# Layer 1's scale and shift by halves behind the last expert, and full fp32 products in gather and combine

## The chip, the cores and the metric

One core of a Trainium2 chip runs the kernel. The metric is the device time of one execution in microseconds (us). A run of the kernel before took 723.83 us in the median of three (722.95 to 725.26). TensorE, VectorE, ScalarE, GpSimd and SyncE are called PE, DVE, ACT, POOL and SP, as the profile calls them. SP issues the weight transfers.

## What is computed

Two layers, 256 tokens of width 1024, all in fp32. Both sub-layers of a layer normalise, scale and shift by vectors made from a conditioning row, and end in a gated residual with another normalisation:

```
for l in range(DEPTH):
    mod = cond @ w_mod[l] + b_mod[l]
    sh1, sc1, g1, sh2, sc2, g2 = split(mod, 6)
    h = layer_norm_plain(x) * (1 + sc1) + sh1
    y = concat(attention(q, k, v), pool(p)) @ w_out[l]      # q, k, v, p = split(h @ w_in[l])
    x = layer_norm_affine(ALPHA * x + g1 * y)
    h = layer_norm_plain(x) * (1 + sc2) + sh2
    y = grouped_moe(h)                                      # 16 experts, top 2 inside one group
    x = layer_norm_affine(ALPHA * x + g2 * y)
```

An expert is silu(h @ w_gate) * (h @ w_up) @ w_down with 512 inner columns. The weights of the 16 experts of one layer are 96 MB, so nearly all that is read from HBM is expert weights.

## The kernel before

**Weights.** `Stream` (line 35) holds a list of transfers in the order of use, mostly 1 MB each. It issues the next one on SP's queue whenever fewer than `limit` tiles are alive in a ring of 21 slots; `free` gives a tile back, `allow` moves the limit. A transfer into a slot waits for the last instruction that read it. The list stands in lines 114 to 169: for layer 0 the mixer's weights, `w_mod` in pieces v = 2, 4, 3, 5 (gate, scale, shift, gate), layer 1's scale piece (v = 1), eight pairs of experts (`add_pair`), and layer 1's shift piece (v = 0).

**Scale and shift.** `mod_mm` (line 290) multiplies the conditioning with one piece of `w_mod` on PE; `mod_fin` (line 327) copies the result, turns it by four PE transposes and reduces it on DVE. For layer 1, `mod_mm(l + 1, 1)` runs on PE in layer 0's mixer, between the two halves of the router's logits (line 719); its `mod_fin` runs in the second expert pair (line 1095). `mod_mm(1, 0)` runs behind the last expert of layer 0 (line 1145). Vectors v = 2, 4 and 3 are made on DVE instead, by `mod_dve` (line 353), eight operations each.

**Entry of layer 1.** `ready(t)` (line 1149) normalises 128 tokens on DVE, `enter` turns all eight 128-column pieces on PE and applies scale and shift on ACT or DVE; then `qk_mm` makes q and k in 16 products of 128x512 for that half of the tokens.

**Experts.** A pair i of experts passes through `gate_up` (line 907), `silu`, `act_t`, `down` (line 951) and `combine` (line 987); `combine(i - 1)` stands in pair i. Products of an expert use 64 columns of PE, so that the two experts of a pair lie side by side. Two calls per layer, `gather(0)` and `gather(4)` (line 868), collect the tokens of eight experts with a one-hot matrix. The normalised tokens are kept as a sum of two parts in float32r, `xh` and `xl`, made in `mixer` (lines 679 and 725 to 727), and each 128x512 product of the gather is made twice, once for each part:

```
for t in range(2):
    for xs in (xh, xl):
        T.matmul(b, xs[:, t, k * 128:(k + 1) * 128], SX[i][t], start=(n == 0), stop=(n == 3))
```

Likewise `down` splits an expert's output into `oh` and `ol` (lines 973 and 974: a cast on ACT and a subtraction on DVE), and `combine_mm` (line 982) multiplies both with the scatter matrix. `past` (line 1053) holds the case of more than 64 tokens on an expert, which this input does not take.

**Names.** In the profile `ps` is a PSUM bank, `wr` a ring slot, `s` a 128x512 work tile, `xn` and `hT` two large tiles that are reused (in the experts they hold `xh` and `xl`), `sT` the scatter matrix. L984 is `combine_mm`, L876 `gather`, L918 `gate_up`, L960 `down`, L455 `qk_mm`, L622 the output projection, L361 `mod_dve`, L297 `mod_mm`.

Of the kernel before, what the change touches and what calls it, by code (L numbers as in the profile page):

```python
# [8 lines left out]
F = mybir.dt.float32  # L9
BF = mybir.dt.bfloat16  # L10
FR = mybir.dt.float32r
# [5 lines left out]
D = 1024  # L17
# [56 lines left out]
def tile_trunk(ctx, tc, x, c, w_mod, b_mod, w_in, w_pool, pool_scale, w_out, ln1_g, ln1_b,  # L74
# [35 lines left out]

    def add_qk(l, q):
        st.add(("in", l, "qk", q), w_in[l].rearrange("(k p) n -> p k n", p=128)[:, 2 * q:2 * q + 2, 0:D])

    def add_in(l):
        w = w_in[l].rearrange("(k p) n -> p k n", p=128)
        if l:
            for q in range(4):
                add_qk(l, q)
# [38 lines left out]
    for l in range(DEPTH):  # L157
# [90 lines left out]
    def bias_cols():  # L248
# [6 lines left out]
        V.tensor_scalar(bcol[:, 0, :, 1], bcol[:, 0, :, 1], 1.0, None, op0=OP.add)  # L255
# [46 lines left out]
    col01 = const.tile([128, 2, 8], F, name="col01")  # L302
    colt[0, 0], colt[0, 1] = col01[:, 0], col01[:, 1]
# [15 lines left out]
    def mod01_fin(h, part):  # L319
# [3 lines left out]
        o = col01[:, :, 2 * h:2 * h + 2]  # L323
        V.reduce_sum(o, b[:, 0:256].rearrange("p (k v o r) -> p v k o r", k=2, v=2, o=2)[:, :, :, :, 0], axis=AX.X)
        V.tensor_add(o, o, bcol[:, 0, 2 * h:2 * h + 2, 0:2].rearrange("p k v -> p v k"))

# [104 lines left out]
    def enter(l, t, hT, xn):  # L431

        for h in range(2):
            b = ps()
            for k in range(4):
                kk = 4 * h + k
                T.transpose(b[:, k * 128:(k + 1) * 128], xn[:, t, kk * 128:(kk + 1) * 128], ident)
            for k in range(4):
# [4 lines left out]
                else:  # L443
                    A.activation(o, i, AF.Identity, scale=colt[l, 1][:, kk:kk + 1], bias=colt[l, 0][:, kk:kk + 1])

    def mixer(l, hT, xn, ready):
        pq = [[ps(), ps()] for _ in range(2)]

        def qk_mm(t, qs=range(4), kks=range(2)):
            for q in qs:  # L450
# [9 lines left out]
        if l:  # L460
            ready(0)
            qk_mm(0)
            ready(1)
        else:
# [11 lines left out]
        for t in range(2):  # L476
            if t:
                qk_mm(1, range(4) if l else (3,))
# [44 lines left out]
        for t in range(2):  # L523
            for n, dst in ((0, qT), (1, kT)):
# [3 lines left out]
                (A.copy if n else V.tensor_copy)(dst[:, :, t * 128:(t + 1) * 128], b.rearrange("p (c s) -> p c s", c=4))  # L528
# [76 lines left out]
        w = slot()  # L605
        xn2 = [w[:, t * D:(t + 1) * D] for t in range(2)]
        xnT = slot().rearrange("p (k s) -> p k s", k=8)
        st.allow(NS - 6)
# [24 lines left out]
        def norms_of(t):  # L633
            z = xn2[t]
# [14 lines left out]
        def turn(t):  # L649
            for h in range(2):  # L650
                b = ps()
                for k in range(4):
                    T.transpose(b[:, k * 128:(k + 1) * 128], xn2[t][:, (4 * h + k) * 128:(4 * h + k + 1) * 128], ident)
# [4 lines left out]
        xh = big.tile([128, 2, D], FR, name="xn")  # L658
# [20 lines left out]
        A.copy(xh[:, 0], xn2[0])  # L679
        mod_dve_fin(l, 3, acc[3])  # L680
        st.allow(NS - 3)
# [531 lines left out]
```

## Time and profile before

| what | value |
|---|---|
| median of 3 runs | 723.83 us |
| the profiled execution's own time | 724.93 us |
| its span, first to last instruction | 723.1 us |
| PE busy | 678.9 us (94%) |
| DVE busy | 326.8 us (45%) |
| ACT busy | 124.8 us (17%) |
| read from HBM | 278.59 MB, 387 GB/s over the span |
| mean granted PE clock | 0.986 |

The profiled execution is 1.1 us above the median. Times in rows count from the start of the span. A matmul's duration in a row is its latency; products that follow each other overlap, so the pace is read from the start of one to the start of the next. In a timeline row the first number is the start, the second the length; "x32" joins 32 records, and the bracket at the end tells how long the engine was idle before it and who released it.

### The profile page before, as it was taken

The page shows a single profiled execution, that of the slowest core. Times are in us where ns is not written, and L with a number is a line of the kernel's source. Part 1 is how long each engine was busy: PE and PEld are TensorE (multiplying, and loading weights), DVE is VectorE, ACT ScalarE, POOL GpSimd, SP SyncE. Part 2 cuts the span into 40 slices and gives each one's busy share as a digit, 9 for nine tenths or more (in the row PEclk, how much of TensorE's full clock was granted, in tenths as well). Part 3 has the DMA queues.
Part 4 walks back from the last instruction along what each step waited for, and adds up shares of the span by engine and source line. Part 5 has one row for each costly group of instructions (what it writes and reads, how often), then busy time and mean ns, then how long its engine had stood idle before and what let it go on. Part 6 is the DMA issues. An engine that isn't in the chain of part 4 may idle for free. (4 is left out here: it accounts for less than half of the span.)

```text
span 723.1 us, 8334 instructions
## 1 busy us (share of the span) xinstructions
PE 678.9 (94%) x3213; PEld 316.8 (44%) x3218; DVE 326.8 (45%) x582; ACT 124.8 (17%) x268; POOL 49.7 (7%) x76
## 2 busy tenths in 40 slices
PE   5999899999999999989979999998999999998994
PEld 2447555553333533423324575555333344342331
DVE  4008897662332532413153966666323243241305
ACT  1011432130110210121002035213210011012100
POOL 5001501100000000000010051010000000000002
PEclk9999999999999999999989999999999999999998
DMA  9999999999999999999999999767699999999992
GB/s 307 366 384 409 408 409 420 373 421 392 424 420 420 422 421 421 420 416 418 395 406 392 409 410 406 310 272 301 282 420 422 421 424 419 420 422 418 418 395 77
DMA packets 61729, 280.37 MB, mean 388 GB/s; under 512 B 5008, under 2 KB 14264, under 8 KB 38632
## 3 DMA queue, kind: packets, MB, share of 16 engines
q1 hardware_dynamic: 61040, 279.20, 96.1%
q8 instruction: 30, 0.49, 0.3%
q10 hardware_dynamic: 312, 0.32, 0.1%
q0 software_dynamic: 320, 0.14, 0.1%
q14 instruction: 27, 0.22, 0.1%
HBM read 278.59 MB, written 1.05 MB: 387 GB/s over the span
## 5 line engine op out<-in xcount | busy, mean ns | idle before, releaser
L918 PE MATMUL ps<-wr 128*64 128x512 f32 x1024 | 226.1, 596 | 0.0
L918 PEld LDWEIGHTS ps<-wr 128*64 128x64 f32 x1024 | 73.5, 138 | 147.2 <-issue 142.3
L960 PE MATMUL ps<-wr,s 128*64 128x512 f32 x512 | 113.8, 595 | 3.7 <-DVE s L945 2.9
L960 PEld LDWEIGHTS ps<-wr,s 128*64 128x64 f32 x512 | 35.5, 137 | 72.0 <-issue 63.8
L970 DVE SCALAR_TENSOR_TENSOR s<-ps,gc,gb 128x512 f32<-128x512 f32 x32 | 24.0, 748 | 84.0 <-PE ps L960 84.0
L455 PE MATMUL ps<-wr,hT 128*128 128x512 f32 x128 | 57.0, 597 | 0.4 <-ACT hT L429 0.2
L361 DVE SCALAR_TENSOR_TENSOR wr<-wr,condT 128x1024 f32<-128x1024 f32 x42 | 55.8, 1329 | 2.3 <-DMA wr<-in_w_mod_dram 0.9
L622 PE MATMUL ps<-wr,hT 128*128 128x512 f32 (+1 forms) x160 | 55.7, 507 | 0.1
L389 POOL TENSOR_TENSOR rs<-rs,mhalf 128x1 f32<-128x1 f32 x16 | 13.2, 823 | 554.1 <-DVE rs L388 554.1
L935 DVE TENSOR_TENSOR s<-s,ps 128x512 f32<-128x512 f32 x16 | 11.0, 687 | 86.5 <-PE ps L918 86.5
L973 ACT CAST wr<-s 128x512 fp32r<-128x512 f32 x30 | 18.5, 618 | 164.7 <-PE ps L918 107.7
L974 DVE TENSOR_TENSOR wr<-s,wr 128x512 fp32r<-128x512 f32 x30 | 20.8, 692 | 55.6 <-ACT wr L973 55.6
L622 PEld LDWEIGHTS ps<-wr,hT 128*128 128x128 f32 x160 | 30.2, 190 | 23.8 <-issue 21.5
L455 PEld LDWEIGHTS ps<-wr,hT 128*128 128x128 f32 x128 | 23.6, 190 | 28.9 <-issue 27.1
L984 PE MATMUL ps<-wr,sT 128*128 128x512 f32 x120 | 33.6, 413 | 0.0
L578 PE MATMUL ps<-wr,hT 128*128 128x512 f32 x64 | 28.3, 595 | 0.0
L504 PE MATMUL ps<-hT,wr 128*128 128x256 f32 x128 | 28.1, 380 | 0.0
L984 PEld LDWEIGHTS ps<-wr,sT 128*128 128x128 f32 x120 | 20.9, 189 | 16.3 <-issue 13.0
L933 DVE SCALAR_TENSOR_TENSOR s<-s,ps 128x512 f32<-128x512 f32 x16 | 11.0, 685 | 36.7 <-ACT s L932 36.7
L504 PEld LDWEIGHTS ps<-hT,wr 128*128 128x128 f32 x128 | 24.2, 190 | 4.5 <-issue 1.3
L876 PE MATMUL ps<-s,xn 128*128 128x512 f32 x64 | 25.4, 398 | 0.3 <-DVE s L854 0.3
L996 DVE TENSOR_TENSOR xt<-xt,ps 128x512 f32<-128x512 f32 x40 | 25.2, 683 | 0.5
(240 smaller groups left out, 611.5 us busy)
## 6 DMA issues: line engine op xcount, KB each, us to landing
wr<-in_w_gate_dram SPq DMA_DIRECT2D x64, 1024.0 KB, 19.3
wr<-in_w_up_dram SPq DMA_DIRECT2D x60, 1024.0 KB, 19.3
wr<-in_w_down_dram SPq DMA_DIRECT2D x56, 1024.0 KB, 19.5
wr<-in_w_mod_dram SPq DMA_DIRECT2D x48, 1024.0 KB, 15.1
wr<-in_w_in_dram SPq DMA_DIRECT2D x16, 1024.0 KB, 15.1
wr<-in_w_out_dram SPq DMA_DIRECT2D x8, 1024.0 KB, 18.7
wr<-in_w_down_dram SPq DMA_DIRECT2D x12, 512.0 KB, 11.1
wr<-in_w_up_dram SPq DMA_DIRECT2D x8, 512.0 KB, 17.4
```

What stands on the lines that cost most here:

```text
L361: V.scalar_tensor_tensor(acc, w[:, kk], condT[:, k, 0:1], acc, op0=OP.mult, op1=OP.add)
L455: T.matmul(pq[t][n], hT[:, k, t * 128:(t + 1) * 128], w[:, kk, n * 512:(n + 1) * 512], start=(k == 0), stop=(k == 7))
L504: T.matmul(pp[g // 2][:, (g % 2) * 256:(g % 2) * 256 + 256], w[:, kk, g * 128:(g + 1) * 128], hT[:, k, :], start=(k == 0 and g % 2 == 0), ...
L578: T.matmul(pv[t], hT[:, k, t * 128:(t + 1) * 128], w[:, kk, :], start=(k == 0), stop=(k == 7))
L622: T.matmul(py[t][-1][:, 0:c1 - c0], catT[:, k, t * 128:(t + 1) * 128], w[:, kk, n * 512 + c0:n * 512 + c1], start=(q == 2 and kk == 0), st ...
L876: T.matmul(b, xs[:, t, k * 128:(k + 1) * 128], SX[i][t], start=(n == 0), stop=(n == 3))
L918: T.matmul(bs[nm][64 * j:64 * j + 64, :], XE[i][k // 4][:, k % 4, c0:c0 + 64], st.get((nm, l, 2 * i + j, q))[:, k - k0, :], start=(k == 0) ...
L960: T.matmul(bo[n][64 * j:64 * j + 64, :], AT[i][:, k, 64 * j:64 * j + 64], st.get(("d", l, 2 * i + j, q))[:, k - k0, (n - n0) * 512:(n - n0 ...
L970: V.scalar_tensor_tensor(o, bo[n], GC[i], g2[:, c0], op0=OP.mult, op1=OP.mult)
L974: V.tensor_sub(ol[:, c0], o, oh[:, c0].bitcast(F))
L984: T.matmul(b, STt[i][:, t * 128:(t + 1) * 128], o[:, n * 512:(n + 1) * 512], start=(start and j == 0), stop=(stop and j == 1), skip_group_ ...
L996: V.tensor_add(b if i == NPAIR - 3 else xt[:, t, c0], xt[:, t, c0], b)
```

## The change

1. Gather and combine (also in `past`) lose the split into two parts: tokens and expert outputs stay fp32 and one fp32 product takes the place of two float32r ones. The two calls that split the tokens on ACT and DVE, and the cast and subtraction behind each expert, go; `down` writes its result straight into a tile `ob`.
2. Layer 1's scale and shift come by halves of 512 columns (both vectors together in `mod1`), all four transfers of a half side by side, both halves behind the last expert pair in the list, with layer 1's q and k weights between. `mod_mm(l + 1, 1)` in layer 0 goes, and PE gets seven `warm` products in that place, as layer 1 has now. `enter` turns and scales one half of the columns at a time, and the q and k products of layer 1 go by quarters.
3. In layer 0, the two copies of turned q behind the PE transposes move from DVE to ACT (`A.copy if n or not l`).
4. The ring's limits go up by one in two places, since the normalised tokens no longer take a slot.

```diff
+    def add_mod1(h):
+        w = w_mod[1].rearrange("(p k) n -> p k n", k=8)
+        for v in (1, 0):
+            for q in range(2):
+                st.add(("m1", h, v, q), w[:, 4 * q:4 * q + 4, v * D + h * 512:v * D + (h + 1) * 512])
...
         add_mod(l, 5)
-        if l + 1 < DEPTH:
-            add_mod(l + 1, 1)
         for i in range(NPAIR):
             add_pair(l, i)
         if l + 1 < DEPTH:
-            add_mod(l + 1, 0)
+            for q in range(4):
+                if q % 2 == 0:
+                    add_mod1(q // 2)
+                add_qk(l + 1, q)
...
+    def mod1(h):
+        acc = ps()
+        for k in range(8):
+            for v in range(2):
+                j = 2 * v + k % 2
+                T.matmul(acc[32 * j:32 * j + 32, :], condT[:, k, :], st.get(("m1", h, v, k // 4))[:, k % 4, :],
+                         start=(k < 2), stop=(k > 5))
+            if k % 4 == 3:
+                for v in range(2):
+                    st.free(("m1", h, v, k // 4))
+        part = s2()
+        A.copy(part, acc)
+        return part
...
         if l:
             ready(0)
-            qk_mm(0)
+            enter(l, 0, 0, hT, xn)()
+            qk_mm(0, (0, 1))
+            part = mod1(1)
             ready(1)
+            enter(l, 1, 0, hT, xn)()
+            mod1_fin(1, part)
+            fins = [enter(l, 0, 1, hT, xn)]
+            qk_mm(1, (0, 1))
+            fins.append(enter(l, 1, 1, hT, xn))
+            for fin in fins:
+                fin()
+            qk_mm(0, (2, 3))
...
-                (A.copy if n else V.tensor_copy)(dst[:, :, t * 128:(t + 1) * 128], b.rearrange("p (c s) -> p c s", c=4))
+                (A.copy if n or not l else V.tensor_copy)(dst[:, :, t * 128:(t + 1) * 128], b.rearrange("p (c s) -> p c s", c=4))
...
-        if l + 1 < DEPTH:
-            mod_mm(l + 1, 1)
         norms_of(1)
         exps(0)
-        if l + 1 == DEPTH:
-            warm(7)
-
-        V.tensor_sub(xl[:, 0], xn2[0], xh[:, 0].bitcast(F))
-        V.tensor_copy(xh[:, 1], xn2[1])
-        V.tensor_sub(xl[:, 1], xn2[1], xh[:, 1].bitcast(F))
+        warm(7)
...
                 for t in range(2):
-                    for xs in (xh, xl):
-                        T.matmul(b, xs[:, t, k * 128:(k + 1) * 128], SX[i][t], start=(n == 0), stop=(n == 3))
-                        n += 1
+                    T.matmul(b, X[:, t, k * 128:(k + 1) * 128], SX[i][t], start=(t == 0), stop=(t == 1))
...
-                    V.scalar_tensor_tensor(o, bo[n], GC[i], g2[:, c0], op0=OP.mult, op1=OP.mult)
-                    if last and n:
-                        break
-                    A.copy(oh[:, c0], o)
-                    V.tensor_sub(ol[:, c0], o, oh[:, c0].bitcast(F))
+                    V.scalar_tensor_tensor(O[i][:, c0], bo[n], GC[i], g2[:, c0], op0=OP.mult, op1=OP.mult)
...
         def combine_mm(i, t, n, b, start=True, stop=True):
-            for j, o in enumerate(O[i]):
-                T.matmul(b, STt[i][:, t * 128:(t + 1) * 128], o[:, n * 512:(n + 1) * 512],
-                         start=(start and j == 0), stop=(stop and j == 1), skip_group_check=not start)
+            T.matmul(b, STt[i][:, t * 128:(t + 1) * 128], O[i][:, n * 512:(n + 1) * 512],
+                     start=start, stop=stop, skip_group_check=not start)
...
-            if i == 1 and l + 1 < DEPTH:
-                mod_fin(l + 1, 1)
```

How the instructions stand now, at three places. First PE in layer 0's second expert pair (`L918`, now `L948`, is gate and up; `L984`, now `L1007`, the combine of the first pair; `L941`/`L971` and `L894`/`L924` transposes; `L335` the transposes of `mod_fin`). Before:

```order
L918 MATMUL ps<-wr 64x512 x32
L984 MATMUL ps<-wr,sT 128x512 x8
L941 MATMUL ps<-ident,s_1356 128x128 x4
L335 MATMUL ps<-ident,s_1381 128x128 x4
L894 MATMUL ps<-ident,s_1299 128x128 x4
L960 MATMUL ps<-wr,s_1379 64x512 x16
```

Now:

```order
L948 MATMUL ps<-wr 64x512 x32
L1007 MATMUL ps<-hT,sT 128x512 x4
L971 MATMUL ps<-ident,s_1311 128x128 x4
L924 MATMUL ps<-ident,s_1254 128x128 x4
L989 MATMUL ps<-wr,s_1330 64x512 x16
```

Eight combine products become four, of fp32, and the four transposes of `mod_fin` are gone. Second, PE where layer 1 makes q and k (`L437`, now `L465`, is `enter`; `L455`, now `L488`, the products; `L339` is `mod1`, `L351` `mod1_fin`). Before:

```order
L437 MATMUL ps<-ident,xn 128x128 x8
L455 MATMUL ps<-wr,hT 128x512 x16
L437 MATMUL ps<-ident,xn 128x128 x8
L455 MATMUL ps<-wr,hT 128x512 x16
L504 MATMUL ps<-hT,wr 128x256 x32
```

Now:

```order
L465 MATMUL ps<-ident,xn 128x128 x4
L488 MATMUL ps<-wr,hT 128x512 x8
L339 MATMUL ps<-wr,condT 32x512 x16
L465 MATMUL ps<-ident,xn 128x128 x4
L351 MATMUL ps<-ident,s_5180 128x128 x4
L465 MATMUL ps<-ident,xn 128x128 x4
L488 MATMUL ps<-wr,hT 128x512 x8
L465 MATMUL ps<-ident,xn 128x128 x4
L488 MATMUL ps<-wr,hT 128x512 x16
L548 MATMUL ps<-hT,wr 128x256 x32
```

The products begin after four transposes, and the second half of scale and shift stands among them. Third, DVE in layer 0's attention (`L745`, now `L777`, ends the rotation of q and k, `L359` and `L361`, now `L388` and `L390`, are `mod_dve`; `L528` the copy of turned q; `L554`/`L598` the mask). Before:

```order
L745 TENSOR_TENSOR xn<-s_463 128x16x8
L359 TENSOR_SCALAR wr<-wr,condT 128x1024
L361 SCALAR_TENSOR_TENSOR wr<-wr,condT 128x1024 x7
L528 COPY wr<-ps 128x4x128 x2
L554 TENSOR_TENSOR ps<-ps,mask 128x512
L555 TENSOR_REDUCE nm<-ps 128x4
```

Now:

```order
L777 TENSOR_TENSOR xn<-s_463 128x16x8
L388 TENSOR_SCALAR wr<-wr,condT 128x1024
L390 SCALAR_TENSOR_TENSOR wr<-wr,condT 128x1024 x7
L598 TENSOR_TENSOR ps<-ps,mask 128x512
L599 TENSOR_REDUCE nm<-ps 128x4
```

The two copies have left DVE's queue, where they stood behind `mod_dve`.

## Rows read from the trace of the kernel before

**Rows 1.** Page, parts 1 and 2: busy times; GB/s in 40 slices.

```profile
PE 678.9 (94%) x3213; PEld 316.8 (44%) x3218; DVE 326.8 (45%) x582; ACT 124.8 (17%) x268; POOL 49.7 (7%) x76
...
GB/s 307 366 384 409 408 409 420 373 421 392 424 420 420 422 421 421 420 416 418 395 406 392 409 410 406 310 272 301 282 420 422 421 424 419 420 422 418 418 395 77
```

**Rows 2.** Groups by form: count | busy us, mean ns | idle before.

```profile
L918 PE MATMUL ps<-wr 128*64 128x512 f32 x1024 | 226.1, 596 | 0.0
...
L984 PE MATMUL ps<-wr,sT 128*128 128x512 f32 x120 | 33.6, 413 | 0.0
```

**Rows 3.** Busy by stretch: length, five engines, PE clock, DMA share, GB/s.

```profile
460.00:520.00 60.00, 56.80 (x332) 31.47 (x333) 34.03 (x73) 14.98 (x28) 4.14 (x4) 1.00 0.67 264
```

**Rows 4.** Timeline of PE: a combine, then a gather's 32 records.

```profile
245.42 2.13 PE L984 MATMUL ps<-wr,sT 128*128 128x512 f32 x8
247.38 0.63 PE L941 MATMUL ps<-ident,s 128*128 128x128 f32 x4
247.77 0.47 PE L876 MATMUL ps<-s,xn 128*128 128x512 f32 x1
...
255.16 0.60 PE L894 MATMUL ps<-ident,s 128*128 128x128 f32 x4
```

**Rows 5.** Timeline of PE: 16 fp32 products of the same shape.

```profile
449.62 13.90 PE L622 MATMUL ps<-wr,hT 128*128 128x512 f32 x32
463.35 0.82 PE L667 MATMUL ps<-ident,wr 128*128 128x128 f32 x6
```

**Rows 6.** Timeline, layer 0's attention, DVE and PE.

```profile
73.79 1.27 DVE L528 COPY wr<-ps 128x512 f32<-128x512 f32 x2
74.62 2.08 PE L534 MATMUL ps<-wr 64*128 64x128 f32 x16 [3.48 <-DVE wr L528]
...
76.77 0.70 DVE L554 TENSOR_TENSOR ps<-ps,mask 128x512 f32<-128x512 f32 x1 [1.70 <-PE ps L534]
...
88.54 9.21 DVE L361 SCALAR_TENSOR_TENSOR wr<-wr,condT 128x1024 f32<-128x1024 f32 x7
...
97.90 1.13 PE L372 MATMUL ps<-ident,wr 128*128 128x128 f32 x8
```

**Rows 7.** Timeline, DVE and PE at the router, layer 0, layer 1.

```profile
140.54 1.23 DVE L646 TENSOR_SCALAR wr<-xt,mv,rs 128x1024 f32<-128x1024 f32 x1 [0.73 <-POOL rs L389]
...
142.76 1.07 PE L653 MATMUL ps<-ident,wr 128*128 128x128 f32 x8
...
489.29 1.20 DVE L646 TENSOR_SCALAR wr<-xt,mv,rs 128x1024 f32<-128x1024 f32 x1 [0.73 <-POOL rs L389]
...
490.63 1.06 PE L653 MATMUL ps<-ident,wr 128*128 128x128 f32 x8 [0.92 <-DVE r_mx L713]
```

**Rows 8.** Timeline of PE, second expert pair, layer 0, layer 1.

```profile
196.52 2.14 PE L984 MATMUL ps<-wr,sT 128*128 128x512 f32 x8
...
201.37 1.08 PE L960 MATMUL ps<-wr,s 128*64 128x512 f32 x4
...
544.26 2.13 PE L984 MATMUL ps<-wr,sT 128*128 128x512 f32 x8
...
547.59 0.65 PE L960 MATMUL ps<-wr,s 128*64 128x512 f32 x2 [0.29 <-ACT s L948]
```

**Rows 9.** Timeline, layer 1's entry; last, `mod_mm` in layer 1's router.

```profile
371.48 0.55 POOL L389 TENSOR_TENSOR rs<-rs,mhalf 128x1 f32<-128x1 f32 x1 [4.29 <-DVE rs L388]
...
372.74 1.93 PE L297 MATMUL ps<-wr,condT 128*32 128x512 f32 x8 [2.49 <-DMA wr<-in_w_mod_dram]
...
378.30 0.80 DVE L1162 TENSOR_SCALAR xn<-xt,mv,rs 128x1024 f32<-128x1024 f32 x1
...
380.43 14.00 PE L455 MATMUL ps<-wr,hT 128*128 128x512 f32 x32
394.27 1.04 PE L437 MATMUL ps<-ident,xn 128*128 128x128 f32 x8
...
484.25 3.62 PE L297 MATMUL ps<-wr,condT 128*32 128x512 f32 x32
```

More of the change, by code (lines that the diff above doesn't have):

```diff
@@ L10 @@
 BF = mybir.dt.bfloat16
-FR = mybir.dt.float32r
 I32 = mybir.dt.int32
@@ L300, in mod_mm @@
         macc[l, v] = acc
-    col01 = const.tile([128, 2, 8], F, name="col01")
-    colt[0, 0], colt[0, 1] = col01[:, 0], col01[:, 1]
+    col01 = const.tile([128, DEPTH, 2, 8], F, name="col01")
+    for l in range(DEPTH):
+        for v in range(2):
+            colt[l, v] = col01[:, l, v]
     def mod01(h):
@@ L429, in enter01_fin, with enter, fin @@
                 A.activation(o, i, AF.Identity, scale=colt[0, 1][:, kk:kk + 1], bias=colt[0, 0][:, kk:kk + 1])
[L431 to L437, printed above, removed]
+    def enter(l, t, h, hT, xn):
+        b = ps()
+        for k in range(4):
+            kk = 4 * h + k
+            T.transpose(b[:, k * 128:(k + 1) * 128], xn[:, t, kk * 128:(kk + 1) * 128], ident)
+        def fin():
             for k in range(4):
@@ L444, in enter @@
                     A.activation(o, i, AF.Identity, scale=colt[l, 1][:, kk:kk + 1], bias=colt[l, 0][:, kk:kk + 1])
+        return fin
     def mixer(l, hT, xn, ready):
-        pq = [[ps(), ps()] for _ in range(2)]
+        pq = [[], []]
         def qk_mm(t, qs=range(4), kks=range(2)):
+            if not pq[t]:
+                pq[t] += ps(), ps()
             for q in qs:
@@ L477, in mixer @@
             if t:
-                qk_mm(1, range(4) if l else (3,))
+                qk_mm(1, (2, 3) if l else (3,))
             A.activation(qk[:, t, 0:512], pq[t][0], AF.Copy, scale=DH ** -0.5)
@@ L604, in mixer @@
         G, B = norm_rows(l, 0)
-        w = slot()
-        xn2 = [w[:, t * D:(t + 1) * D] for t in range(2)]
+        xn2 = big.tile([128, 2, D], F, name="xn")
         xnT = slot().rearrange("p (k s) -> p k s", k=8)
-        st.allow(NS - 6)
+        st.allow(NS - 5)
         py = [[], []]
@@ L730, in mixer @@
         exps(1)
-        return xh, xl, (mx, ex, sm), gate
+        return xn2, (mx, ex, sm), gate
     def rope(qk):
@@ L838, in router, with experts @@
         return posm, rest
-    def experts(l, xh, xl, posm, rest):
+    def experts(l, X, posm, rest):
         sc2, sh2 = colt[l, 4], colt[l, 3]
@@ L846, in experts @@
         XB = [[], []]
+        ob = big.tile([128, 2, D], F, name="hT")
         def onehot(i):
@@ L1012, in over @@
                 for k in range(4):
-                    m = 0
                     for t in range(2):
-                        for xs in (xh, xl):
-                            T.matmul(pb[:, k * 128:k * 128 + n], xs[:, t, (4 * h + k) * 128:(4 * h + k + 1) * 128], Sx[:, t, 0:n],
-                                     start=(m == 0), stop=(m == 3))
-                            m += 1
+                        T.matmul(pb[:, k * 128:k * 128 + n], X[:, t, (4 * h + k) * 128:(4 * h + k + 1) * 128], Sx[:, t, 0:n],
+                                 start=(t == 0), stop=(t == 1))
                 for k in range(4):
@@ L1144, in tile_trunk @@
         else:
-            mod_mm(l, 0)
+            part0 = mod1(0)
             warm(3)
@@ L1150, in ready @@
                 b = tiny.tile([128, 2, 6], F, name="bn")
-                if not t:
-                    own.append(ends(0))
+                own.append(ends(t))
                 for n in range(2):
@@ L1158, in ready @@
                 if not t:
-                    mod_fin(l, 0)
+                    mod1_fin(0, part0)
                     warm(8)
-                    own.append(ends(1))
-                V.tensor_scalar(xn[:, t], xt[:, t], mv[:, 0:1], rs, op0=OP.subtract, op1=OP.mult)
-                enter(l, t, hT, xn)
-        xh, xl, mes, gate = mixer(l, hT, xn, ready)
-        r = router(l, mes, gate)
-        ends, norm, norm_aside = experts(l, xh, xl, *r)
+                for n in range(2):
+                    V.tensor_scalar(xn[:, t, n * 512:(n + 1) * 512], xt[:, t, n * 512:(n + 1) * 512],
+                                    mv[:, 0:1], rs, op0=OP.subtract, op1=OP.mult)
+        x2, mes, gate = mixer(l, hT, xn, ready)
+        ends, norm, norm_aside = experts(l, x2, *router(l, mes, gate))
     rest = xt[:, 1, 512:D]
```

39 lines of the change are left out of this document (19 added, 20 removed).

## The prediction

> **What bounds the kernel now.** I read the page's busy times and slices first. PE is busy 94% of the span, and the transfers run at about 420 GB/s in most slices [rows 1], so either could set the end. Two views separate them. In the groups by form, the products of gate and up and those of the combine show no idle time before them [rows 2]: PE does not wait for weights there. In the busy time by stretch, the transfers fall to 264 GB/s between 460 and 520 us while PE is busy 56.8 of 60 us [rows 3]: the weights then wait for free slots, that is for PE. At 420 GB/s these 60 us would have moved 9.4 MB more. So from layer 0's experts on, PE's own products set the time, with a few stalls between the stages, and every microsecond added to PE counts unless it falls into a stall.
>
> **The price of the products.** A gather leaves 32 records from 247.77 to 255.16, a combine eight from 245.42 to 247.38 [rows 4]: 0.231 and 0.245 us for one float32r product. Sixteen fp32 products of the same shape, 128 rows by 128 columns by 512, leave 32 records in the output projection, from 449.62 to 463.35 [rows 5]: 0.429 us a record, and two records a product, so 0.858 us. One fp32 product thus takes the place of two that took 0.46 to 0.49 us.
>
> Gather: 13.73 − 7.39 = 6.34 us for each of four calls, 25.4 us. Combine: the eight records become four products, 8 × 0.429 = 3.43 us, so 1.47 us more; 120 records [rows 2] are 15 such groups, 22.1 us. If the 120 records are priced by their busy time of 33.6 us instead, which holds the latency at each group's end, it is 51.5 − 33.6 = 17.9. I take 21, nearer to the pace, since groups split in two hand over once more. The upper end prices the new products by the row's length, 14.00 of the q and k products [rows 9]: 0.4375 a record, 26.4 + 23.1. So **46.4 us, between 43.3 and 49.5.** None of it finds cover, since PE has no idle time in the experts.
>
> Four short products would be 0.92 or 0.98 us, and the sum 29.6 + 29.4 = 59.0 us; the row of full products of the same shape is only 3.5 to 3.7 short ones long, and I take the row. The Trainium skill, FP8 and Floating Point Precision, TensorE Precision Notes, states that true fp32 takes four passes through the array. By that rule on this case's short records it would be the 59.0; the trace agrees in kind and is 6 to 12% cheaper.
>
> **What the change gives back.**
> *Layer 0's attention.* DVE ends its eight operations of `mod_dve` at 73.79, makes the two copies of q that PE waits 3.48 us for, idles 1.70 us, and begins the mask at 76.77 [rows 6]. With the copies on ACT (17% busy [rows 1]) PE can go on before 73.79, and the mask starts there, 3.0 us earlier. From the mask DVE is a chain up to the second `mod_dve`, which ends at 97.75, and PE's transposes of its result follow at 97.90 [rows 6]. PE gains more ahead of that, but waits for this chain: 3.0 us (0 if ACT is late, 3.5 if all of PE's wait goes).
> *Layer 0's router.* PE turns the second half of the tokens 0.99 us after DVE has them (141.77 to 142.76), since `mod_mm(1, 1)` stands before it; in layer 1, which already has seven warm products there, 0.14 us [rows 7]. The three splitting operations on DVE, now gone, are hidden behind the transposes and logits, up to some 0.1 us. 0.9 us (0 to 1).
> *Second expert pair.* From the combine to the down products layer 0 takes 4.85 us, layer 1, with no `mod_fin` there, 3.33 [rows 8]: 1.5 us (0.5 to 1.9).
> *Entry of layer 1.* PE waits 2.49 us for the last tile of the shift [rows 9], and the transposes and products stand behind it. Now the first half of scale and shift is 3.6 us of products by the row of the same shape (484.25 [rows 9]), its tiles are there (below), and the normalisation decides: POOL ends at 372.03. From the start of the normalised tile to the first product it was 378.30 to 380.43, 2.1 us; by halves, 0.4 less. So the first product stands at about 374.0 instead of 380.4. From there, q and k were 2 × 13.84 + 1.0 = 28.7 us; now 27.7, plus the second half's 3.6, three groups of four transposes (half of 1.04 each) and those of `mod1_fin`, 2.1, and 0.3 for the copy they wait for: 33.7. The end moves from 409.1 to 407.7: 1.4 us (−1 to 5).
> *Beside other work.* The casts and subtractions behind the experts (DVE 45%, ACT 17% busy [rows 1]) hid behind PE's products; with slower products the cover only grows. No expert product waited for them: nothing.
> Sum: 3.0 + 0.9 + 1.5 + 1.4 = **6.8 us**.
>
> **Transfers.** Their bytes stay. Layer 0's experts get 4 MB earlier what they need; behind them stand 8 MB of scale and shift with q's and k's weights. Before, the last of 4 MB landed at 372.7 when PE wanted it some 3 us earlier. By then PE will be late by half of 46 us, less 5, about 17 us, which at 400 GB/s is 6.8 MB; the 4 MB more take 10.5 us. So nothing should wait, and `mod_dve` in layer 1, whose tiles come after, has the same lead.
>
> **Sum.** 46.4 − 6.8 = 39.6 us. The span of 723.1 becomes 762.7; the profiled execution's 724.93 becomes 764.5; that execution was 1.1 us above the median, so against 723.83 I predict **763.4 us**, 5.5% slower.
>
> **The rivals.**
> *Savings that do not come.* New waits at the entry of layer 1 (its tokens now pass PE, ACT and DVE in quarters) or on ACT eat the 6.8 us: 770.2. For it: seven stages change order. Against it: each saving is a wait with a row. Chance 0.06.
> *Late halves.* If the list stalls on ring slots late in layer 0, so that the lead above is lost, the 4 MB more cost 10.5 us: 773.9. It decides from the point where the transfers' start slips by over 6 us. For it: a slower PE frees slots later. Against it: the slots of the last pair's gate and up products are freed well before PE needs the halves. Chance 0.05.
> *Four full passes.* Each full product costs four short ones, because its weight load or its operands (a one-hot, a scatter matrix) keep the short pace: 59.0 − 6.8 = 52.2 more, 776.0. The row of the same shape [rows 5] speaks against it. Chance 0.04. It is what the page named above would give.
> *The transfers set the end* (the other side). If PE waits for weights unseen, as matmul records with modelled ends could hide, the longer products cost nothing up to the transfers' pace: a pair's 12.6 MB take 29.9 us at 420 GB/s, and that is the point from which it decides. Then only the savings remain: 717.0. For it: 420 GB/s in nearly all slices [rows 1]. Against it: the drop at 460 to 520 [rows 3], and the groups without idle time [rows 2]. Chance 0.04.
> *It does not do what it says.* If one fp32 product ran as one short record, gather and combine would halve: 29.5 less, and 6.8, so 687.5. The 32 records for 16 products [rows 5] speak against it. Chance 0.01.
>
> **The numbers.** The forecast has 0.80. Its own range, with the bounds of the price and of the savings (0.5 to 10), is 757 to 772; it takes in the first rival. The late halves, the four passes and the two faster cases stay outside, 0.14 together. So it is my range. About 0.3%, 2.2 us, is what a measurement of this kernel tells from no change. Faster by over 0.3%: 0.05, the two faster cases. Within: 0.01. Slower: 0.94.
>
> **What would show it.** Right: a gather at 13.7 us and a combine of four products at 3.4 us in PE's timeline; layer 0's mask some 3 us earlier; no wait for a transfer at layer 1's entry; 33 to 34 us from its first q and k product to the last; transfers at less than 420 GB/s in the experts, since the ring is full. Wrong: gathers shorter than 13 us, PE idle in front of gate and up products, waits for the scale and shift tiles, or a total below 757.

## The result and the profile after

The changed kernel takes **765.73 us**, median of 4 runs (763.9 to 766.86), against 724.24 us (722.95 to 725.26) for the kernel before: ratio 1.0571, 95% interval 1.0543 to 1.06. It is slower by 41.5 us; the prediction was 763.4 us, 757 to 772. The profiled execution took 763.9 us, with a span of 762.1 us (before 723.1).

The page of the changed kernel, as in [rows 1]: busy times, the granted clock, and GB/s in 40 slices.

```profile
PE 722.4 (95%) x3225; PEld 315.1 (41%) x3225; DVE 305.6 (40%) x546; ACT 105.2 (14%) x238; POOL 50.5 (7%) x76
...
PEclk9999999999999999999999999999999999999997
...
GB/s 308 365 390 409 409 415 419 397 87 422 421 418 419 421 418 420 419 415 388 332 393 395 409 409 420 304 366 22 393 419 419 419 419 420 420 420 416 402 100 55
```

PE is busy 43.5 us longer, DVE 21.2 us and ACT 19.6 us less: the casts and subtractions of the split are gone, and no gain from that shows in the stretches below. Two slices of the transfers, the ninth and the 28th, have fallen to 87 and 22 GB/s.

The groups by form (count, busy us and mean ns of a record, idle time before), as in [rows 2]:

```profile
L948 PE MATMUL ps<-wr 128*64 128x512 f32 x1024 | 223.4, 593 | 0.0
...
L1007 PE MATMUL ps<-hT,sT 128*128 128x512 f32 x128 | 60.2, 605 | 0.0
L907 PE MATMUL ps<-s,xn 128*128 128x512 f32 x128 | 55.7, 593 | 0.3 <-DVE s L887 0.3
```

The combine's records take 60.2 us, against 33.6 [rows 2] and 3.8 us for the last pair's products, which were fp32 before too (`L980`), so 22.8 us more. The number of the gather's records has stayed at 128, each longer. The timeline of PE shows the four products of a group and the gather behind it, which began at 245.42 and 247.77 before [rows 4]:

```profile
249.97 3.70 PE L1007 MATMUL ps<-hT,sT 128*128 128x512 f32 x8
253.51 0.63 PE L971 MATMUL ps<-ident,s 128*128 128x128 f32 x4
253.98 8.32 PE L907 MATMUL ps<-s,xn 128*128 128x512 f32 x19
```

The four products take 3.54 us from first start to the next line's start (1.96 before). The four gathers take 13.90, 13.74, 13.90 and 13.74 us, 25.4 us more than before.

The timeline of PE at layer 1's entry, which answers to [rows 9]:

```profile
384.19 3.64 PE L339 MATMUL ps<-wr,condT 128*32 128x512 f32 x32
...
390.78 0.62 PE L465 MATMUL ps<-ident,xn 128*128 128x128 f32 x4
391.96 7.13 PE L488 MATMUL ps<-wr,hT 128*128 128x512 f32 x16 [0.55 <-ACT hT L474]
399.02 3.64 PE L339 MATMUL ps<-wr,condT 128*32 128x512 f32 x32
...
404.35 7.03 PE L488 MATMUL ps<-wr,hT 128*128 128x512 f32 x16
411.22 0.60 PE L465 MATMUL ps<-ident,xn 128*128 128x128 f32 x4
411.66 13.90 PE L488 MATMUL ps<-wr,hT 128*128 128x512 f32 x32
425.39 1.89 PE L548 MATMUL ps<-hT,wr 128*128 128x256 f32 x8
```

No wait for a transfer is left. PE comes to the entry at 384.19, 18.1 us later than before (366.12), and leaves q and k at 425.39: 41.2 us, against 43.1.

Where the 39.0 us of span lie, from the starts of the same lines in both traces (the third column is a run of the next section):

| stretch of PE | before | changed kernel | products alone |
|---|---|---|---|
| start to layer 0's first gather | 151.8 | 148.4 | 151.6 |
| layer 0's experts | 214.3 | 235.8 | 238.9 |
| layer 1's entry, up to the end of q and k | 43.1 | 41.2 | 37.4 |
| from there to layer 1's first gather | 90.3 | 90.3 | 90.3 |
| layer 1's experts | 212.8 | 235.6 | 237.4 |

The profiled execution of the third column was 2.0 us above its kernel's median: behind both branches past the overflow code its 32 products took 8.71 us, where the changed kernel's took 7.02, so each of its two expert rows holds 1.7 us that are not the products' price. The sum looks like the prediction's. The third row of numbers does not: with the products alone the entry is shorter than with the whole change. The experiments go into that.

### The profile page after: what moved, and what is told of

The parts are those of the page before. It is cut to its first block, busy times and chain, and to the rows that moved or that the text cites. A ratio compares the mean times of both kernels' runs of the same rounds, so it can differ in the third digit from the quotient of the medians.

```text
span 762.1 us, 8250 instructions
## 1 busy us (share of the span) xinstructions
PE 722.4 (95%) x3225; PEld 315.1 (41%) x3225; DVE 305.6 (40%) x546; ACT 105.2 (14%) x238; POOL 50.5 (7%) x76
## 3 DMA queue, kind: packets, MB, share of 16 engines
HBM read 278.59 MB, written 1.05 MB: 367 GB/s over the span
## 5 line engine op out<-in xcount | busy, mean ns | idle before, releaser
L948 PE MATMUL ps<-wr 128*64 128x512 f32 x1024 | 223.4, 593 | 0.0
L948 PEld LDWEIGHTS ps<-wr 128*64 128x64 f32 x1024 | 73.0, 137 | 146.6 <-issue 141.5
L1007 PE MATMUL ps<-hT,sT 128*128 128x512 f32 x128 | 60.2, 605 | 0.0
L998 DVE SCALAR_TENSOR_TENSOR hT<-ps,gc,gb 128x512 f32<-128x512 f32 x32 | 24.0, 751 | 89.5 <-PE ps L989 87.7
L488 PE MATMUL ps<-wr,hT 128*128 128x512 f32 x128 | 57.1, 596 | 0.8 <-ACT hT L474 0.5
L390 DVE SCALAR_TENSOR_TENSOR wr<-wr,condT 128x1024 f32<-128x1024 f32 x42 | 55.8, 1329 | 2.3 <-DMA wr<-in_w_mod_dram 0.9
L907 PE MATMUL ps<-s,xn 128*128 128x512 f32 x128 | 55.7, 593 | 0.3 <-DVE s L887 0.3
L907 PEld LDWEIGHTS ps<-s,xn 128*128 128x128 f32 x128 | 24.0, 190 | 30.0 <-issue 27.3
L1007 PEld LDWEIGHTS ps<-hT,sT 128*128 128x128 f32 x128 | 22.6, 190 | 33.1 <-issue 31.2
L962 ACT ACTIVATE s<-ps 128x512 f32<-128x512 f32 x16 | 9.6, 603 | 189.0 <-PE ps L948 189.0
L488 PEld LDWEIGHTS ps<-wr,hT 128*128 128x128 f32 x128 | 23.5, 190 | 28.6 <-issue 26.6
L1019 DVE TENSOR_TENSOR xt<-xt,ps 128x512 f32<-128x512 f32 x40 | 27.5, 687 | 10.4 <-PE ps L1007 10.4
L910 DVE TENSOR_SCALAR wr<-ps,col,col 128x512 f32<-128x512 f32 x16 | 13.0, 810 | 44.4 <-PE ps L907 44.4
```

Of the source, the lines that this page charges most:

```text
L390: V.scalar_tensor_tensor(acc, w[:, kk], condT[:, k, 0:1], acc, op0=OP.mult, op1=OP.add)
L488: T.matmul(pq[t][n], hT[:, k, t * 128:(t + 1) * 128], w[:, kk, n * 512:(n + 1) * 512], start=(k == 0), stop=(k == 7))
L907: T.matmul(b, X[:, t, k * 128:(k + 1) * 128], SX[i][t], start=(t == 0), stop=(t == 1))
L910: V.tensor_scalar(o, b, sc2[:, k:k + 1], sh2[:, k:k + 1], op0=OP.mult, op1=OP.add)
L948: T.matmul(bs[nm][64 * j:64 * j + 64, :], XE[i][k // 4][:, k % 4, c0:c0 + 64], st.get((nm, l, 2 * i + j, q))[:, k - k0, :], start=(k == 0) ...
L998: V.scalar_tensor_tensor(O[i][:, c0], bo[n], GC[i], g2[:, c0], op0=OP.mult, op1=OP.mult)
```

## The experiments

Theory: the longer products on PE are the price, and the other parts give back what the prediction names. Rivals: the transfers take part, as the halves' late tiles or as a bound right behind PE.

### The halves without the products

The halves of scale and shift, and layer 0's copies of q on ACT (the line moves two copies, one for each half of the tokens; the expectations call them the second copy), with the split in two float32r parts and the ring's limits left as they were:

```diff
-        if l + 1 < DEPTH:
-            add_mod(l + 1, 1)
...
+            for q in range(4):
+                if q % 2 == 0:
+                    add_mod1(q // 2)
+                add_qk(l + 1, q)
...
+            part = mod1(1)
             ready(1)
...
```

> The kernel before with everything of the change but the fp32 products: scale and shift of layer 1 by halves behind the last expert, q's second copy on ACT, the tokens and the experts' outputs still split in two float32r parts. Theory 1 (PE's pace sets the time, only the longer products cost, the rest gives back some 7 us): 724.2 - 7 = 717, between 715 and 719, with layer 0's mask 2.4 to 3 us earlier, the router 1 us, the second pair 1.5 us, layer 1's entry 1.4 to 1.9 us shorter. Theory 2 (late halves: without the slow products the transfers have no lead at layer 1's entry; the 4 MB more between the last expert and the second half of q and k land when PE wants them or later): PE waits 2 to 5 us for the tiles of the second half, total 719.5 to 723. Theory 3 (new waits at the entry, whatever the transfers do): 724 or more.

And the same with q's copies left on DVE:

> As the run with the halves and ACT's copy, but with q's second copy left on DVE: only scale and shift by halves (with the warm products in layer 0's router that take the place of the moved ones). Theory 1: 724.2 - 0.9 (router) - 1.5 (second pair) - 1.4 to 1.9 (entry) = 720 to 720.5, so 2.4 to 3 us above the run with both. Theory 2 (late halves): the tiles of the second half land as late as PE wants them or later, the gains ahead of the entry are lost in a wait there: 722 to 725.

Measured: 735.06 us with ACT's copy (before 722.92; ratio 1.0175, 1.0151 to 1.0199), 737.79 us without it (1.0207, 1.0184 to 1.023). The halves by themselves cost 14.9 us, and 12.1 us with ACT's copy, far above theories 1 and 2; the open end of theory 3 holds the number, and a run below shows that its reason is not the cause. ACT's copy makes the 2.7 us that were expected. The busy time by stretch (columns as in [rows 3]) of the run with both at 150 to 170 us:

```profile
150.00:160.00 10.00, 10.00 (x47) 6.09 (x47) 5.45 (x14) 4.79 (x6) 0.00 (x0) 1.00 0.15 60
160.00:170.00 10.00, 10.00 (x49) 3.19 (x46) 0.91 (x2) 0.60 (x1) 0.00 (x0) 1.00 0.93 370
```

And of the kernel before:

```profile
150.00:160.00 10.00, 9.35 (x45) 6.62 (x47) 4.82 (x9) 3.79 (x5) 0.00 (x0) 1.00 1.01 424
160.00:170.00 10.00, 10.00 (x48) 3.30 (x46) 3.38 (x12) 1.81 (x3) 0.00 (x0) 1.00 0.92 360
```

Before, the router used up the scale's 4 MB just ahead of the experts, and the slots that it freed kept the queue going. Without them the ring is full of experts' tiles, none of which comes free before the first pair is under way, and the queue stands: 364 GB/s for 10 us are 3.6 MB, 8.7 us at 420 GB/s. From there to the entry the transfers run without a gap (415 to 421 GB/s from 180 to 340 us), so these 8.7 us are not made up before it. PE's timeline at the entry and DVE's behind it, of the run with both, show who waits:

```profile
366.22 5.99 PE L340 MATMUL ps<-wr,condT 128*32 128x512 f32 x32 [4.28 <-DMA wr<-in_w_mod_dram]
...
405.10 0.75 DVE L389 TENSOR_SCALAR wr<-wr,condT 128x1024 f32<-128x1024 f32 x1 [6.96 <-DMA wr<-in_w_mod_dram]
...
431.21 1.06 PE L572 MATMUL ps<-ident,xn 128*128 128x128 f32 x8 [3.89 <-DVE xn L787]
```

PE waits 4.28 us for the first half's first tile, and its 32 products take 5.92 us in place of 3.57. `mod_dve`, which runs on DVE from 397.29 in the kernel before, waits for its tiles until 405.10; the rotation of q and k stands behind it on DVE, and PE behind that. PE's wait of 3.89 us is as long as what the rotation of the first half of the tokens loses by running beside POOL (5.2 in place of 1.3 us, last section). The first gather of layer 1 begins 9.2 us later than before, at 508.77. So the late tiles of the prediction's rival are real, in a place it did not name too, and what decides is not a slower PE but whether PE is late enough.

### The products without the halves

The fp32 products in gather and combine alone. The slot that the split needed falls free with it, and this run has the limits raised by one too (part 4 of the change):

```diff
-                    for xs in (xh, xl):
-                        T.matmul(b, xs[:, t, k * 128:(k + 1) * 128], SX[i][t], start=(n == 0), stop=(n == 3))
-                        n += 1
+                    T.matmul(b, X[:, t, k * 128:(k + 1) * 128], SX[i][t], start=(t == 0), stop=(t == 1))
...
-            for j, o in enumerate(O[i]):
-                T.matmul(b, STt[i][:, t * 128:(t + 1) * 128], o[:, n * 512:(n + 1) * 512],
-                         start=(start and j == 0), stop=(stop and j == 1), skip_group_check=not start)
+            T.matmul(b, STt[i][:, t * 128:(t + 1) * 128], O[i][:, n * 512:(n + 1) * 512],
+                     start=start, stop=stop, skip_group_check=not start)
...
```

> The kernel before with the fp32 products alone: gather and combine take the whole tokens and outputs in one full fp32 product each, no split, nothing else moved. Theory 1: the price alone, 25.4 us for the gathers and 21 to 23 us for the combines: 724.2 + 46.4 to 48.5 = 770.6 to 772.7; less up to 2.5 us, because the wait for the last shift tile at layer 1's entry has to go when PE comes 24 us later there: 768 to 772.7. The change as a whole must then lie 3 to 7 us under it. Rival (the rest of the change gives nothing, the price is smaller than thought): 765 to 766, like the whole change.

Measured: 766.15 us against 722.92, ratio 1.0595 (1.0568 to 1.0621): 43.2 us, all that the whole change costs. That is the rival's total, but not by its reason: the price is no smaller. PE's timeline at the entry of this run:

```profile
390.50 3.64 PE L296 MATMUL ps<-wr,condT 128*32 128x512 f32 x32
...
397.83 1.09 PE L436 MATMUL ps<-ident,xn 128*128 128x128 f32 x8 [0.60 <-DVE xn L1140]
399.03 14.00 PE L454 MATMUL ps<-wr,hT 128*128 128x512 f32 x32
```

The shift's 32 products pass in 3.57 us, which took 8.49 before with the 2.49 us wait in them [rows 9], and from the entry to the end of q and k it is 37.4 us in place of 43.1. PE comes 24 us later, the tiles are there, and 5.8 us of the price are covered. The 2.49 us were not the only wait of the kernel before, which has one more in front of it:

```profile
369.19 1.07 PE L297 MATMUL ps<-wr,condT 128*32 128x512 f32 x8 [1.15 <-DMA wr<-in_w_mod_dram]
```

Behind them PE ran at a granted clock of 0.63 from 372.7 to 380.4 us, the lower level for most of it; in this run it is 1.00 from the entry on. So 3.6 of the 5.8 us are waits, and the rest is for the most part the clock that fell after them.

The same with the gathers alone changed:

> The kernel before with the fp32 products in the gathers alone; the combine stays in two float32r parts. The gathers cost 4 x 6.34 = 25.4 us more. Theory A (PE's lateness takes away layer 1's entry's wait for the shift, 5.8 us in the run with all fp32 products): 722.9 + 25.4 - 5.8 = 742.5, and the entry some 5.8 us shorter. Theory PE (every microsecond counts in full): 748.3.

Measured: 742.64 us (ratio 1.0273, 1.0247 to 1.0298), 0.1 us from theory A, and its entry takes 37.4 us too, with the limits as before, so part 4 is not what shortens it (part 4 was not tried by itself). The cover is used up by the first 25 us; the combine on top then costs its whole price, 766.15 − 742.64 = 23.5 us.

### One line: layer 0's copies of q on ACT

```diff
-                (A.copy if n else V.tensor_copy)(dst[:, :, t * 128:(t + 1) * 128], b.rearrange("p (c s) -> p c s", c=4))
+                (A.copy if n or not l else V.tensor_copy)(dst[:, :, t * 128:(t + 1) * 128], b.rearrange("p (c s) -> p c s", c=4))
```

> The kernel before with one line of the change alone: the second copy of q in layer 0 goes to ACT in place of DVE. Theory 1 (PE waits for DVE there, and nothing later holds the gain back): the mask starts 2.4 to 3 us earlier and the time falls by as much, 721.2 to 721.8. Rival (the transfers hold it back: they run at 421 GB/s from 170 to 340 us and PE waits for the last shift tile at layer 1's entry, so PE only comes there earlier and waits longer): same mask, but the wait at layer 1's entry grows from 2.5 to about 5 us and the time stays within 1 us of 724.2.

Measured: 721.61 us, ratio 0.9984 (0.9967 to 1.0). DVE's timeline has the mask at

```profile
73.78 0.69 DVE L554 TENSOR_TENSOR ps<-ps,mask 128x512 f32<-128x512 f32 x1
```

which is 3.0 us earlier than in [rows 6]; the transposes behind `mod_dve` begin at 95.54 instead of 97.90, and the first gather 2.35 us earlier. The time falls by 1.3 us, with 2.4 us just at the interval's end and no gain at the other. The gain in the trace is plain, its size in the median is not settled. The rival's longer wait is not there: PE's waits for the shift's tiles at layer 1's entry sum to 4.1 us (3.6 before). In the router's last part, at 140 to 150 us, the transfers already ran at 419 GB/s (381 before).

### The whole change, and the change without the halves

> The changed kernel once more, beside the next one. If the other parts of the change give nothing on top of the fp32 products, it lies within 1 us of 766 (the run with the products alone); if they give what the prediction says (6.8 us on top of a price of 46.4 us), 763 or less with the products alone at 769 to 770.

> The kernel before with the fp32 products and ACT's copy of q, without the halves. In the trace of the run with the products alone layer 1's entry takes 37.5 us, in the changed kernel 41.4 us; against that the changed kernel is 1.5 us shorter in the second pair and 0.9 us in layer 0's router. Theory A (with the fp32 products PE comes late enough to find the shift's tiles there, so the halves only bring their products from a place with slack to the entry, and give back 2.4 of 3.9 us): this kernel is 1 to 2 us faster than the whole change, 763.5 to 764.5 if the change is at 765.5. Rival (the halves gain): it is 2 to 4 us slower than the whole change.

Measured side by side, before at 723.55 us: the whole change 766.21 us (1.0588, 1.0567 to 1.061), without the halves 763.77 us (1.0559, 1.0538 to 1.058). The whole change lies where the products alone lie, and without the halves it is 2.4 us faster. That is what theory A of the last expectation said. The two intervals overlap a little, so the size is loose; the stretches of the traces speak for less: without the halves the entry takes 37.3 us, with them 41.2, and router and second pair give 2.6 us of that back, which leaves 1.2 to 1.3.

### The scale early, the shift by halves

```diff
+        for q in range(2):
+            st.add(("m1", h, q), w[:, 4 * q:4 * q + 4, h * 512:(h + 1) * 512])
...
         if l + 1 < DEPTH:
             add_mod(l + 1, 1)
...
         if l + 1 < DEPTH:
-            add_mod(l + 1, 0)
+            for q in range(4):
+                if q % 2 == 0:
+                    add_mod1(q // 2)
+                add_qk(l + 1, q)
...
```

> The kernel before with q's second copy on ACT, and at layer 1's entry only the shift by halves: its first half stands behind the last expert, its second half behind the first two tiles of q and k; the scale stays in layer 0's router, with its 4 MB ahead of the experts' weights. Theory A (found in the runs of the first call: between 160 us and layer 1's entry the transfers are the bound, and the halves cost 12 us because moving the scale's 4 MB behind the experts leaves the queue idle at 150 to 170 us, when the ring is full): here the queue loses nothing, PE wants 2 MB in place of 4 MB when it comes to the entry, so the wait of 2.5 us there goes and the first q and k product stands 4 to 6 us earlier; less 2.3 us for the second half's products and transposes: 722.9 - 1.3 (ACT's copy, as measured) - 2 to 4 = 717.5 to 720. Theory B (the entry by halves is itself what costs, by its order of tokens): 727 or more.

Measured: 723.44 us against 722.99, ratio 1.0001 (0.9976 to 1.0025), in runs that spread widely, 719.63 to 727.71. Neither theory's number, but the cause of the 12 us is told apart from the order of tokens: ACT's copy and the order of tokens at the entry are those of the first run, the scale stays early, and so 2 MB in place of 4 MB stand before each half of the products. The loss is gone, and the queue does not stop:

```profile
150.00:160.00 10.00, 9.83 (x47) 6.64 (x47) 5.01 (x9) 4.40 (x6) 0.00 (x0) 1.00 1.01 423
```

In the profile the first q and k product stands at 373.38 (before 380.43) and the end of q and k at 406.64 (409.25), 2.6 us earlier, of which 2.1 are left at the end of the span (721.0 against 723.1). The medians show nothing of it, and the kernel's runs spread over 8 us, so whether it is a gain stays open.

### PE slower, where the transfers are the bound

The first run with 36 products without use put into two of layer 0's expert pairs:

```diff
+            if not l and i in (2, 5):
+                warm(18)
             silu(i)
```

> The run with halves and ACT's copy (735.06 us), with 36 products without use (some 0.24 us each, 8.6 us of PE in all) put into layer 0's third and sixth expert pair. Theory A (there the transfers set the end, PE only waits for them at layer 1's entry): the added 8.6 us are hidden, PE's wait of 4.3 us and the drips in the halves' products go, total 734 to 737. Theory PE (PE sets the time in layer 0's experts): 743 to 744.

Measured: 742.79 us (1.0266, 1.0238 to 1.0294): by the total, theory PE. The traces say otherwise. The 36 products took 7.4 us; PE left q and k at 412.45, 2.1 us later than without them, and reached layer 1's first gather 2.4 us later. As much, 2.2 us, it was late already at layer 0's first gather, ahead of all 36 (150.75 against 148.50). So at least 5 of the 7.4 us were hidden, and by these two traces nearly all, as theory A had it. The other 5.7 us arose in layer 1, where nothing was changed, at the branch past the overflow code. PE's timeline there:

```profile
667.88 7.04 PE L960 MATMUL ps<-wr 128*64 128x512 f32 x32
682.55 1.86 PE L438 MATMUL ps<-rowz,selz 128*128 128x512 bf16 x4 [7.63 <-PEq L1100]
684.35 8.71 PE L960 MATMUL ps<-wr 128*64 128x512 f32 x32
```

And in the kernel before:

```profile
656.14 7.04 PE L918 MATMUL ps<-wr 128*64 128x512 f32 x32
665.35 1.02 PE L408 MATMUL ps<-rowz,selz 128*128 128x512 bf16 x4 [2.17 <-PEq L1058]
666.30 7.09 PE L918 MATMUL ps<-wr 128*64 128x512 f32 x32
```

PE stood 7.63 us at the branch in place of 2.17 (2.18 in the first run), and ran at a granted clock of 0.57 from 676 to 688 us, the lower level for most of it; its next 32 products took 8.71 in place of 7.09 us by the rows' lengths. Why the branch took longer in this program was not tried.

### PE faster

One part of the split left out of gather and combine:

```diff
-                    for xs in (xh, xl):
-                        T.matmul(b, xs[:, t, k * 128:(k + 1) * 128], SX[i][t], start=(n == 0), stop=(n == 3))
-                        n += 1
+                    T.matmul(b, xh[:, t, k * 128:(k + 1) * 128], SX[i][t], start=(t == 0), stop=(t == 1))
...
-            for j, o in enumerate(O[i]):
-                T.matmul(b, STt[i][:, t * 128:(t + 1) * 128], o[:, n * 512:(n + 1) * 512],
-                         start=(start and j == 0), stop=(stop and j == 1), skip_group_check=not start)
+            T.matmul(b, STt[i][:, t * 128:(t + 1) * 128], O[i][0][:, n * 512:(n + 1) * 512],
+                     start=start, stop=stop, skip_group_check=not start)
```

> The kernel before with the second part of the split left out of gather and combine (the low bits of tokens and outputs are missing from the result): half of the short products go, 14.8 us of PE in each layer. Theory PE: 722.9 - 29.5 = 693. Theory A (transfers set the end up to layer 1's entry, PE from there): layer 0's 14.8 us turn into a longer wait at layer 1's entry, layer 1's count: 708, between 706 and 712. Theory transfers alone: within 2 us of 722.9.

Measured: 719.77 us, ratio 0.9965 (0.9946 to 0.9983). Of 29.5 us taken from PE (124 short products by the pace of [rows 4]) 3.2 come back, close to the theory of the transfers alone. The waits of PE from 495 to 720 us:

```profile
PE ps L916 <- DMA wr<-in_w_gate_dram: 3.4, 3, 1.3
PE ps L408 <- PEq L1055: 2.8, 1, 2.8
```

From 520 to 690 us the transfers run at 420 GB/s without a gap, and PE now waits for gate's weights, which it did not before [rows 2]. Theory A was right that layer 0's 14.8 us are lost (its experts take 210.8 us in place of 214.3, and q and k end 1.8 us earlier), though part of them already go in the experts and not only at the entry. It was wrong for layer 1, where it let PE have its 14.8 us: from the first gather to the last down products it is 198.6 us in place of 202.5.

### An attempt at a faster kernel

> An attempt at a faster kernel: the shift by halves and ACT's copy (the run at 723.4 us), with tokens and outputs in one float32r part alone (their low bits are left out), and the tile saved by that as one more ring slot for the weights. If before is balanced, PE at its own pace right ahead of the transfers (leaving out the second part brought 3 of 29.5 us, since the transfers took over), one more slot of 1 MB is worth up to 2.5 us of transfers in each layer, and the entry with 2 MB in place of 4 MB another 2 to 5 us: 708 to 716. Rival (PE's pace alone): 693. Rival (the total of the transfers' bytes at their rate, which no slot changes): 718 to 720.

The edit joins the two runs above, keeps the rounded tokens where the second part lay, and raises two limits of the list by one slot:

```diff
-        st.allow(NS - 6)
+        st.allow(NS - 5)
...
-        st.allow(NS - 3)
+        st.allow(NS - 2)
...
```

Measured: 720.04 us, ratio 0.9957 (0.9941 to 0.9973), at the upper edge of the last rival's range. At 460 to 520 us the transfers move 308 GB/s in place of the 294 of leaving out one part alone, 0.8 MB more and so about the slot's worth, but the whole is no faster than that run. With all bits kept, nothing here beat the kernel before by more than ACT's copy, whose interval reaches 1.0.

## Why the prediction was right, and which steps were not

**What bounds the kernel** was half of it. "From layer 0's experts on, PE's own products set the time": upwards yes, the gather run and the products run cost their products but for 5.8 us. Downwards no: 29.5 us less of PE brought 3.2. The drop to 264 GB/s [rows 3] was read rightly as a full ring, but it is a reserve of 9.4 MB for that stretch alone; in both layers' experts the transfers run at their rate. The rival "the transfers set the end" holds as soon as PE gets faster, and the prediction's own figures had it there: it put the point of decision at 29.9 us for a pair, and by [rows 8] and [rows 4] PE passes two pairs in 48.9 us, 24.5 each. In the experts PE is thus the quicker of the two. An estimate: layer 0's eight pairs are 100.7 MB (the 96 MB given ahead count in 2^20 bytes; two layers are 201 of the 278.59 MB read, 72% and not nearly all), and its 214.3 us at 420 GB/s are 90 MB, so 11 MB must lie in the ring when they begin, and this lead is used up about where layer 1's entry comes.

**The price** was 46.4 us; it is 25.4 + 22.8 = 48.2 us by the records, inside its bounds. The gathers came out to the decimal. The combine was mis-sized at 21: the upper end, 23.1, priced by the row of q and k (0.4375 us a record), was the nearer one, since a group of eight new records took 3.54 us, 0.44 each. One full product here is 3.5 to 3.7 of the short float32r ones, and 4.0 of the bf16 products without use of the run with PE slower, which follow each other at 0.217 us: a float32r product, at 0.231 to 0.245 us, is more than a quarter of a full one. The rule of the Trainium skill (FP8 and Floating Point Precision, TensorE Precision Notes), four passes for true fp32, thus agrees with this case when a pass is taken as a bf16 product; the prediction's 59.0 us came of taking a float32r product for one.

**None of it finds cover** failed, and with it the reason that the prediction gave, that PE has no idle time in the experts: the cover lay behind them. 5.8 us were covered at layer 1's entry, as the run with the products alone shows. The prediction had seen that wait and PE's lateness, but booked its end to the halves.

**The attention**, 3.0 us: the mask came 3.0 us earlier, the transposes behind the chain 2.4 us (95.54 for 97.90). **The router**, 0.9: 1.0. **The second pair**, 1.5: it takes 4.85 us as before, with four fp32 products in it that are 1.6 us longer, so 1.6 saved.

**The entry**, 1.4 us: 1.9 in the trace, and wrongly explained. The lateness saves 5.8 us with or without halves; the halves then add the scale's products and more transposes, 3.8 us of PE. Against 2.6 us from router and second pair, they cost more than they give. The prediction's 33.7 us from first to last q and k product is 33.4 in the trace, so its working of the new order was right, and its comparison was not: it should have been made against the old order with the wait gone, and not against the old order as it stood.

**The transfers**: "late by about 17 us" was 18.1, and no tile came late. The 20 us from 150 on moved 1.6 MB, and at 360 to 380 us the rate was 325 GB/s: the ring was full again ahead of the entry. The rival "late halves" missed only because the products made PE late; its price of 10.5 us stands beside 12.1 us for the halves with ACT's copy and 14.9 without, in which part is DVE's wait in `mod_dve`. One of the prediction's signs came only in places: it wanted less than 420 GB/s in the experts, and from 170 to 340 us the rate is 419 (421 before); it falls only around each layer's first gather (the slices of 87 and 22 GB/s) and at 360 to 380 us.

**Not predicted**: behind the branch in layer 0 the profiled execution of before ran at the granted clock 0.79 (318 to 326 us), that of the changed kernel at 1.00 (333 to 341 us), and the 32 products there took 8.71 and 7.02 us from their first start to the next line's:

```profile
319.87 8.78 PE L918 MATMUL ps<-wr 128*64 128x512 f32 x32
328.58 1.20 PE L984 MATMUL ps<-wr,sT 128*128 128x512 f32 x4
```

```profile
335.74 7.09 PE L948 MATMUL ps<-wr 128*64 128x512 f32 x32
342.75 1.98 PE L1007 MATMUL ps<-hT,sT 128*128 128x512 f32 x4
```

It is no part of the change: profiled once more, the changed kernel took 8.71 us behind layer 1's branch, where it had taken 7.02 the first time. The slower stretch in the kernel before made the spans' difference 1.7 us smaller.

The sum of the profiled executions: 48.2 − 2.4 − 1.0 − 1.6 − 1.9 − 1.7 = 39.6, and 39.0 was measured. That this is the prediction's 39.6 again is luck: the 1.8 us of the combine are offset by the 1.7 of the clock. Without the clock it is 41.3, and the medians are 41.5 us apart. The total was nearly right because two misses had the same cause: what was booked as the halves' gain was cover for the products, and the halves' own gain was nothing.

## What to carry to other kernels

Where PE and the transfers are within a few per cent of one another, price every edit in both directions: what PE gains may only be a longer wait at the next place where it meets the transfers, and a loss may be covered there. A list of weights behind a ring of slots loses its lead wherever the ring fills with tiles that nobody can use yet; early tiles that are soon consumed keep it moving, and moving them late can cost their transfer time although no byte is added. And compare a new order with the old one under the same lateness, or the wait that goes anyway is booked to the edit.

## What the runs showed of the hardware

An fp32 product of 128 x 128 x 512 leaves two records that follow each other at 0.43 to 0.44 us, whether its operands are weights, a one-hot or a scatter matrix; no difference between these operands shows in its time. Four bf16 products of this shape take as long, 0.217 us each.

At the branch past the overflow code PE stands idle for 1.9 to 2.2 us in the kernel before and in the changed one, but for 7.63 us at layer 1's branch of one program, in which only layer 0 had been given more products. Behind the branch the granted clock falls in some executions of one and the same kernel (32 products in 8.71 us) and not in others (7.02).

In the first run rotation and pooling came to overlap. An operation of DVE with two operands in SBUF took 2.08 us beside one of POOL of 2.65 us, where it takes 0.28 us alone, and ended 0.15 us behind it. DVE's and POOL's timeline:

```profile
425.04 2.65 POOL L791 TENSOR_TENSOR wr<-wr 128x1084 f32<-128x1084 f32 x1 [8.65 <-ACT wr L558]
...
425.76 2.08 DVE L782 TENSOR_TENSOR s<-xn,cs 128x128 f32<-128x128 f32 x1
...
427.76 0.28 DVE L783 TENSOR_TENSOR s<-xn,cs 128x128 f32<-128x128 f32 x1
427.77 1.66 POOL L792 TENSOR_TENSOR wr<-wr 128x807 f32<-128x807 f32 x1
```

The Trainium skill, SBUF — State Buffer, Who interferes with whom, names such a pair: a DVE operation with two inputs in SBUF and a GpSimd operation that reads SBUF contend for a port that they share, and one shuts the other out. The rows agree: the rotation of the first half of the tokens took 5.2 us there, and 1.3 us in the kernel before, where POOL stood still.
